# A hybrid decoder step on one core: a sample's value window put together in DRAM, parts of the first tokens ahead of their squares, constants cast later

## The chip, the core and the metric

The kernel runs on one core of a Trainium2 chip. The core has TensorE (PE; its weight loads are shown apart as PEld), VectorE (DVE), ScalarE (ACT), GpSimd (POOL) and SyncE (SP). In this kernel SP computes nothing: it issues all the DMAs of the program, in one queue. 16 DMA engines move the data. The metric is device time in microseconds (us), lower is better; a result is the median of several runs.

## The reference

One inference step of a two-layer trunk with model width 1024, for a prompt of 2048 tokens behind 16 learned meta tokens, and for 8 sample sequences of one token each. Layer 0 projects the normed input and feeds two branches: attention in a window of 128 with a learned sink for each head, and a gated delta rule in chunks behind a short convolution; both are gated and projected together. Layer 1 is gated linear attention. What the change touches is the samples' attention in layer 0. Its window is the 128 youngest keys and values; the oldest of the cache drops out and the new one comes in, and the window that is used is also an output:

```python
    k = jnp.concatenate([k_buf.astype(k_new.dtype), k_new], axis=1)
    v = jnp.concatenate([v_buf.astype(v_new.dtype), v_new], axis=1)
    ...
    mask = (diff >= 0) & (diff < WINDOW)
    o = _sink_attend(q.reshape(Bn, T, A_KV_HEADS, A_GROUP, A_HEAD_DIM), k, v, mask, sink)
    return o.reshape(Bn, T, A_HEADS, A_HEAD_DIM), k[:, T:], v[:, T:]
```

So for each of the 8 samples the value window is rows 1 to 127 of its cache and one new row, each row 128 numbers of float32 (512 bytes).

## The kernel before

The tokens are cut into four groups of 512 columns; the first also carries the 8 sample tokens and the 16 meta tokens in front (536 columns, `CMAX`). For each group the kernel runs layer 0 and layer 1 (`ab_head`, `ab_rest`, `c_main`, `c_out`). Every large product is made of three: weights and activations are split into a rounded part (`hi`, on ACT) and the rest (`lo`, on DVE), and hi x hi, hi x lo and lo x hi are summed in PSUM. In the first group the weights come raw from DRAM and are split (`load_w`, L270 to L278), and their parts are stored in DRAM (L245) for the later groups, which load them (L258). Eight buffers (`NW`) hold weights, and each block of 128 output columns takes three of them: raw, hi, lo. Four PSUM buffers (`pp`) take the large products, four others (`pc`) the small ones. General tiles in SBUF come from a ring of 52 (`ft`).

The order of emission is written by hand. `bulk` emits the large products and between them steps of side streams (generators that yield an estimated wait), chosen by a clock of estimated PE time: delta-rule chunks (`dn_head`), pairs of attention heads (`swa_pair`), the samples' work (`dn_sample`, `swa_extra`). `join` emits what is left of streams before going on. Dependences and semaphores are set by the framework, which also reorders instructions: one that is ready early may be issued ahead of others on its engine, and so do loads that need nothing. On each engine, and in SP's DMA queue, the order so found is then fixed: what stands behind a waiting instruction waits too.

The start (L132 to L226). The gains `PV`, the first eight x tiles `X0`, the first weights `w0` and the constants `CC` are loaded. A loop over the eight tiles makes hi (ACT, L149) and lo (DVE, L150) and adds the squares into `acc0` (ACT L152 or L155, DVE L156). Then small constants are cast or computed: `identb`, `negb` and `triu` (masks and identity in other types), `nsink`, `nea` (an exponential on ACT, L183), `WU` (three steps from the loaded `w_gku`) and `SEL`. `ab_first` makes the row scales `rbn` from `acc0`; `ab_head` then projects K (`ab_k`), whose results are multiplied by `rbn` and copied into the key tiles `kh`, and starts the first convolution head (`ab_conv`), in which the value projection `ab_v` runs.

The samples' values. In `ab_v` (slot "e") the values of the 24 extra tokens are evicted to `e` (named `exv`); `vm` and a part of `BA` are copied from it by DMA (L701, L702), and `vs` (8 partitions x 128) by DVE (L705). `swa_extra` runs beside the last head pair of the first group. It loads, for two halves of four samples, the key window `kc` (transposed, 128 partitions, L495) and the value window `vc`, where the partition is the position in the window: 127 partitions from the cache (L498), the 128th from `vs` (L499). It then computes scores (L527), copies them (L531), softmax, transposes (L542), multiplies by `vc` and stores the result as columns of `M`. Last, it writes the output `vs`: 127 rows from cache to output (L563) and the new row (L564).

Behind it `ab_out` makes the output projection in two parts: first the heads that are ready (`kts[0]`, two of eight, 256 columns of weights), with the residual x loaded by L991 and added in the eviction (`ev_1`, a line of the helper at L115), then, after `join(q.dn + q.sw + xs)`, the other six (`ev_2`).

Of the kernel before, what the change touches and what calls it, by code (L numbers as in the profile page):

```python
# [9 lines left out]
F32 = mybir.dt.float32  # L10
# [10 lines left out]
SMP = 8  # L21
# [47 lines left out]
def kernel(ctx: ExitStack, tc: tile.TileContext, ins, outs):  # L69
# [16 lines left out]
    def const(shape, dt=F32, name="c"):  # L86
        n = nm(name)
        return cp.tile(shape, dt, tag=n, name=n)

    def ft(dt=F32, shape=(128, CMAX)):  # L90
        return wk.tile(list(shape), dt, tag="T", bufs=NT, name=nm("t"))
# [19 lines left out]
    def TT(out, a, b, op, eng=None):  # L111
        (eng or V).tensor_tensor(out, a, b, op=op)  # L112

    def STT(out, a, s, b, op0, op1):
        V.scalar_tensor_tensor(out, a, s, b, op0=op0, op1=op1)  # L115

    def TS(out, a, s1, s2=None, op0=ALU.mult, op1=None):
        if op1 is None:
            V.tensor_scalar(out, a, s1, None, op0=op0)  # L119
        else:  # L120
            V.tensor_scalar(out, a, s1, s2, op0=op0, op1=op1)
# [24 lines left out]
    for kt in range(8):  # L146
        hi, lo = hl(), hl()
        gk = PV[:, P_GAB + kt:P_GAB + kt + 1]
        A.activation(hi, X0[kt], AF.Copy, scale=gk)  # L149
        STT(lo, X0[kt], gk, hi.bitcast(F32), mul, sub)  # L150
        if kt == 0:
            A.activation(acc0, X0[kt], AF.Square)  # L152
        else:
            sq = ft()
            A.activation(sq, X0[kt], AF.Square)  # L155
            TT(acc0, acc0, sq, add)  # L156
        H0[0].append(hi)
        H0[1].append(lo)
    RV = const([128, 16], name="RV")
    SY.dma_start(RV, ins["rowv"].to_broadcast([128, 16]))  # L160
    ident = CC[:, C_ID:C_ID + 128]
# [4 lines left out]
    idc = CC[:, C_IDC:C_IDC + 32]  # L166
    mrow = CC[:, C_MR:C_MR + 1]
    identb = const([128, 128], BF16, "identb")
    V.tensor_copy(identb, ident)
    negb = const([128, 128], BF16, "negb")  # L170
    ngr = ft(shape=(128, 128))
    SY.dma_start(ngr, ins["negm"])
    V.tensor_copy(negb, ngr)
    triu = const([128, 128], U32, "triu")
    V.tensor_copy(triu, tri)
    ones = const([128, 128], name="ones")
    V.memset(ones, 1.0)
    mh = const([128, 1], name="mh")
    V.memset(mh, -0.5)
    nsink = const([128, 8], name="nsink")  # L180
    TS(nsink, RV[:, 0:8], -1.0)
    nea = const([128, 4], name="nea")
    A.activation(nea, RV[:, 8:12], AF.Exp)  # L183
    TS(nea, nea, -1.0)
    dtb = RV[:, 12:16]

    def rpow(out, x):
        G.tensor_tensor(out, x, mh[0:x.shape[0]].to_broadcast(list(x.shape)), op=ALU.pow)  # L188


    WU = const([96, 512], F32R, "WU")
    wur = ft(shape=(128, 512))
    SY.dma_start(wur[0:16, :], ins["w_gku"])
    V.memset(WU.bitcast(F32), 0.0)
    V.tensor_copy(WU[0:16], wur[0:16, :])
    V.tensor_copy(WU[32:48], wur[0:16, :])
    TT(WU[64:80], wur[0:16, :], WU[0:16].bitcast(F32), sub)


    Sdn = []  # L200
# [14 lines left out]

    GS = GR = const([96, 640], F32R, "GS")
    V.memset(GS.bitcast(F32), 0.0)
    SEL = const([96, 4], F32R, "SEL")
    V.memset(SEL.bitcast(F32), 0.0)
    V.tensor_copy(SEL[0:4], ident[0:4, 0:4])  # L220
    V.tensor_copy(SEL[32:36], ident[32:36, 32:36])
    junk = const([128, 256], BF16, name="junk")

    AMK = const([128, 4, 128], name="AMK")
# [246 lines left out]
    def swa_extra(q, gx):  # L471
        vt = q.vt

        vm, vs = vt["m"], vt["s"]
        sc = cb()
        for h in range(8):
            MM(sc[0:16, 16 * h:16 * h + 16], QX[:, h, SMP:EX], KX[:, h // 4, SMP:EX])
        S3 = t512((128, 8, 16))[0:16]
        TT(S3, sc[0:16, 0:128].rearrange("p (h k) -> p h k", h=8), bcm(CC[0:16, C_MSK + 128:C_MSK + 144], 8), add)
        st = sm((128, 32))[0:16]  # L480
        V.tensor_reduce(st[:, 0:8], S3, axis=AX.X, op=amax)
        TT(st[:, 0:8], st[:, 0:8], RV[0:16, 0:8], amax)
        TT(S3, S3, bc(st[:, 0:8], 16), sub)
        A.activation(S3, S3, AF.Exp)
        TT(st[:, 8:16], RV[0:16, 0:8], st[:, 0:8], sub)
        A.activation(st[:, 8:16], st[:, 8:16], AF.Exp)
        V.tensor_reduce(st[:, 16:24], S3, axis=AX.X, op=add)
        TT(st[:, 16:24], st[:, 16:24], st[:, 8:16], add)
        V.reciprocal(st[:, 24:32], st[:, 16:24])
        TT(S3, S3, bc(st[:, 24:32], 16), mul)  # L490
        yield from take_in("T", 5)
        kc, vc = ([ft(shape=(128, 4, 128)) for _ in range(2)] for _ in range(2))
        for x in range(2):
            b4 = slice(4 * x, 4 * x + 4)
            SY.dma_start(kc[x][:, :, 0:127], ins["kcT"][:, b4])  # L495
            for kv in range(2):
                V.tensor_copy(kc[x][64 * kv:64 * kv + 64, :, 127], KX[:, kv, 4 * x:4 * x + 4])
            SY.dma_start(vc[x][0:127], ins["cv"][b4, 1:128, :].rearrange("b k d -> k b d"))  # L498
            SY.dma_start(vc[x][127:128, :, :], vs[4 * x:4 * x + 4, :])  # L499
        QZ = ft(shape=(128, 512))  # L500
        V.memset(QZ, 0.0)
        for kv in range(2):
            r = slice(64 * kv, 64 * kv + 64)
            dst = QZ[r, 0:504].rearrange("p (b x) -> p x b", x=72)[:, 4 * kv:4 * kv + 4, :]
            V.tensor_copy(dst, QX[:, 4 * kv:4 * kv + 4, 0:7])
            V.tensor_copy(QZ[r, 504 + 4 * kv:508 + 4 * kv], QX[:, 4 * kv:4 * kv + 4, 7])
        yield LAT["sx_1"], 0.3
        pt = cb()
        for h in range(8):
            T.transpose(pt[0:16, 16 * h:16 * h + 16], S3[:, h, :], ident[0:16, 0:16])  # L510
        PT = t512((128, 128))[0:16]
        A.copy(PT, pt[0:16, 0:128])
        yield LAT["sx_2"], 0.3
        po = cb()
        for kv in range(2):
            MM(po[64 * kv:64 * kv + 64, 0:64], vm[0:16, 64 * kv:64 * kv + 64], PT[:, 64 * kv:64 * kv + 64])
        yield from until(lambda: gx)
        for u in range(4):
            z = t512((128, 16))
            TT(z, po[:, 16 * u:16 * u + 16], GX[:, u, SMP:EX], mul)  # L520
            store_m0(q, u, z, SMP, META)

        yield 0.5, 0.1

        sc = cb()
        for b in range(8):
            MM(sc[0:64, 0:128], QZ[:, 64 * b:64 * b + 64], kc[b // 4][:, b % 4], start=(b == 0), stop=(b == 7))  # L527
        P = t512((128, 128))[0:64]
        st = sm((128, 8))[0:64]
        snk = PV[0:64, P_SNK:P_SNK + 1]  # L530
        V.tensor_copy(P, sc[0:64, 0:128])  # L531
        V.tensor_reduce(st[:, 0:1], P, axis=AX.X, op=amax)
        TT(st[:, 0:1], st[:, 0:1], snk, amax)
        TS(st[:, 1:2], st[:, 0:1], -1.0)
        A.activation(P, P, AF.Exp, bias=st[:, 1:2], accum_out=st[:, 2:3])
        A.activation(st[:, 3:4], snk, AF.Exp, bias=st[:, 1:2])
        TT(st[:, 2:3], st[:, 2:3], st[:, 3:4], add)
        V.reciprocal(st[:, 4:5], st[:, 2:3])
        TS(P, P, st[:, 4:5])
        yield LAT["sx_3"], 0.9  # L540
        pt = cb()
        T.transpose(pt[:, 0:64], P, ident[0:64, 0:64])  # L542
        PT = t512((128, 64))
        A.copy(PT, pt[:, 0:64])
        yield LAT["sx_4"], 0.1
        po = cb()
        for b in range(8):
            MM(po[:, 8 * b:8 * b + 8], vc[b // 4][:, b % 4], PT[:, 8 * b:8 * b + 8])
        pos = t512((128, 64))
        A.copy(pos, po[:, 0:64])  # L550
        pv = pos.rearrange("p (b h) -> p h b", b=8)
        for u in range(4):
            z = t512((128, 8))
            for kv in range(2):
                r = slice(64 * kv, 64 * kv + 64)
                TT(z[r], pv[r, 4 * kv + u, :], GX[r, u, 0:SMP], mul)
            store_m0(q, u, z, 0, SMP)

        give("T", 5)
        yield LAT["sx_5"], 0.9  # L560

        SY.dma_start(outs["ks"][:, 0:127, :], ins["ck"][:, 1:128, :])
        SY.dma_start(outs["vs"][:, 0:127, :], ins["cv"][:, 1:128, :])  # L563
        SY.dma_start(outs["vs"][:, 127, :], vs[0:8, :])  # L564
        kt_ = cb()
        for kv in range(2):
            T.transpose(kt_[0:8, 64 * kv:64 * kv + 64], KX[:, kv, 0:SMP], ident[0:64, 0:64])
        kn = t512((128, 128))[0:8]
        A.copy(kn, kt_[0:8, 0:128])
        SY.dma_start(outs["ks"][:, 127, :], kn)  # L570
# [110 lines left out]
    def ab_v(q):  # L681
# [7 lines left out]
        def ev_v(p2, slot):  # L689
# [6 lines left out]
            if slot == "e":  # L696
# [6 lines left out]
                V.tensor_copy(BA[0:SMP, 5, :], e[0:SMP, 128:136])  # L703
                vs = wk.tile([128, 128], F32, tag="va", bufs=6, name=nm("vs"))
                V.tensor_copy(vs[0:SMP], e[0:SMP, 0:128])  # L705
                q.vt["m"], q.vt["s"] = vm, vs
            else:
                t = wk.tile([128, 128], F32, tag="va", bufs=6, name=nm("va"))
# [250 lines left out]

    def ab_head(q):  # L960
        bulk(ab_k(q))
        ab_conv(q, 0)

    def ab_rest(q):
# [914 lines left out]
```

## Time and profile before

| | |
|---|---|
| median of 3 runs | 2248.47 us (2241.6 to 2253.84) |
| the profiled execution | 2245.83 us |
| its span in the profile | 2244.0 us |
| busy share of PE, PEld | 96%, 81% |
| busy share of DVE, ACT, POOL | 55%, 37%, 12% |
| DMA, mean | 178 GB/s |
| granted PE clock, mean | 0.985 |

The page of the profile gives one execution. Busy shares are averages over the span; the span in 40 slices of 56 us shows where an engine is less busy:

```profile
PE   7899987999999999999999999999999999999997
...
PEclk9999998999999999999999999999999999999998
```

Each digit is the busy share, and the clock that was granted to PE, in tenths. The slices that matter here are the first and those from 280 to 390 us (the sixth and seventh), all in the first group. In the views that follow L12 is a line of the kernel; L109, L112, L115, L119 and L121 are helpers (`MM`, `TT`, `STT`, `TS`), so their rows are told apart by the tiles they write and read. "SPq" rows are DMA issues of SP with the time that the issue held its queue, not the transfer.

### The profile page before, as it was taken

How to read it: one execution, taken by the hardware profiler on the slowest of the kernel's cores; microseconds unless marked ns; L12 is line 12 of the kernel's file. 1: busy time of each engine (PE TensorE's matmuls, PEld its weight loads, DVE VectorE, ACT ScalarE, POOL GpSimd, SP SyncE). 2: the span in 40 equal slices, each digit the busy share in tenths (PEclk: the TensorE clock that was granted, in tenths of full speed). 3: DMA queues.
4: the chain of work that ended last, by engine and by line, in shares of the span. 5: the costliest groups of instructions: out<-in, count | busy, mean ns of one | idle time of the engine just before them, and what ended most of it. 6: DMA issues, size and time to landing. Idle time of an engine off the chain costs nothing.

```text
span 2244.0 us, 43751 instructions
## 1 busy us (share of the span) xinstructions
PE 2155.2 (96%) x17290; PEld 1809.1 (81%) x17290; DVE 1231.4 (55%) x3501; ACT 836.4 (37%) x2235; POOL 264.3 (12%) x314
## 2 busy tenths in 40 slices
PE   7899987999999999999999999999999999999997
PEld 6788877988888877788887877778887877778886
DVE  6778865665565466545344466544335366654323
ACT  4445443443353244334333244334233233334222
POOL 0011100021200011002130110002130001001111
PEclk9999998999999999999999999999999999999998
DMA  6553425858766732364554743274554653274444
GB/s 215 187 193 130 155 84 182 298 181 285 256 229 219 259 120 98 126 216 168 188 186 154 251 141 114 89 253 152 177 187 158 227 176 115 78 257 159 159 147 155
DMA packets 162568, 399.65 MB, mean 178 GB/s; under 512 B 22010, under 2 KB 54426, under 8 KB 162346
## 3 DMA queue, kind: packets, MB, share of 16 engines
q1 hardware_dynamic: 162362, 396.84, 52.0%
q8 instruction: 136, 2.23, 0.4%
q14 instruction: 70, 0.57, 0.1%
HBM read 296.67 MB, written 101.17 MB: 177 GB/s over the span
## 4 chain that ended last, share of the span: by engine, by line
PE 68%; DVE 5%; DMA 2%; issue 2%; ACT 2%; POOL 1%; SPq 0%; DVEq 0%; POOLq 0%; ACTq 0%
PE pp L109 51%; PE pc L109 13%; DVE t L115 2%; DVE t L112 1%; DVE inv L112 1%; PE pc L931 1%; PE pc L1710 1%; DMA t<-x2d 1%; POOL sm L188 0%; DMA t<-in_xT 0%; DVE t L119 0%; DMA raw<-in_w_cv 0%; DVE t L915 0%; DMA raw<-in_w_co 0%; ACT t L920 0%
## 5 line engine op out<-in xcount | busy, mean ns | idle before, releaser
L109 PE MATMUL pp<-t,wh 128*128 128x512 f32 (+1 forms) x4528 | 1267.7, 364 | 32.8 <-DVE t L115 13.3
L109 PEld LDWEIGHTS pp<-t,wh 128*128 128x128 f32 x4528 | 782.1, 190 | 144.6 <-DVE t L115 14.1
L109 PE MATMUL pp<-t,wl 128*128 128x512 f32 (+1 forms) x2264 | 810.4, 359 | 3.1 <-DVE wl L112 3.1
L109 PEld LDWEIGHTS pp<-t,wl 128*128 128x128 f32 x2264 | 430.0, 190 | 62.9 <-DVE wl L112 3.8
L112 POOL TENSOR_TENSOR t<-t,t 128x512 fp32r<-128x512 f32 (+3 forms) x128 | 163.7, 1295 | 526.4 <-ACT t L587 295.2
L109 PE MATMUL pp<-wh,t 128*128 128x256 f32 (+1 forms) x1088 | 208.6, 288 | 3.8 <-DVE QKt L112 3.8
L115 DVE SCALAR_TENSOR_TENSOR t<-t,PV,t 128x512 f32<-128x512 f32 (+4 forms) x232 | 176.7, 769 | 59.4 <-ACT t L1012 26.7
L109 PEld LDWEIGHTS pp<-wh,t 128*128 128x128 f32 x1088 | 171.8, 190 | 6.1 <-DVE QKt L112 4.0
L115 DVE SCALAR_TENSOR_TENSOR t<-pp,t 128x512 f32<-128x512 f32 (+3 forms) x160 | 93.2, 586 | 135.8 <-PE pp L109 64.9
L188 POOL TENSOR_TENSOR sm<-sm,mh 128x2 f32<-128x2 f32 (+3 forms) x84 | 68.5, 815 | 825.3 <-DVE sm L115 373.0
L109 PE MATMUL pp<-wl,t 128*128 128x256 f32 (+1 forms) x544 | 155.4, 286 | 0.0
L112 DVE TENSOR_TENSOR wl<-raw,wh 128x512 fp32r<-128x512 f32 (+3 forms) x138 | 92.3, 688 | 22.3 <-ACT wh L275 11.3
L109 PEld LDWEIGHTS pp<-wl,t 128*128 128x128 f32 x544 | 103.4, 190 | 0.7
L275 ACT CAST wh<-raw 128x512 fp32r<-128x512 f32 (+2 forms) x122 | 67.7, 587 | 77.3 <-DMA raw<-in_w_c 20.7
L112 DVE TENSOR_TENSOR t<-t,t 128x512 f32<-128x512 f32 (+4 forms) x103 | 62.9, 613 | 40.4 <-ACT t L399 38.7
L112 DVE TENSOR_TENSOR QKt<-pp,t 128x512 f32<-128x512 f32 (+1 forms) x40 | 23.2, 586 | 111.6 <-PE pp L109 101.0
L109 PEld LDWEIGHTS pc<-t,t 128*128 128x128 f32 (+4 forms) x496 | 63.0, 162 | 23.4 <-ACT t L1507 5.1
L920 ACT ACTIVATE t<-t,sm 128x257 f32<-128x257 f32 x128 | 64.1, 504 | 45.0 <-DVE sm L115 44.2
L109 PE MATMUL pc<-t,t 128*128 128x128 f32 (+5 forms) x496 | 78.0, 267 | 2.4 <-ACT t L1507 1.1
L399 ACT ACTIVATE t<-t 128x512 f32<-128x512 f32 (+1 forms) x70 | 44.1, 630 | 90.2 <-DVE t L115 67.5
L112 DVE TENSOR_TENSOR t<-pp,t 128x268 f32<-128x268 f32 (+1 forms) x90 | 44.5, 496 | 53.3 <-PE pp L109 38.2
L933 ACT COPY t<-pc 128x512 f32<-128x512 f32 x64 | 37.4, 585 | 75.1 <-PE pc L931 74.9
(334 smaller groups left out, 2808.5 us busy)
## 6 DMA issues: line engine op xcount, KB each, us to landing
wh<-wd SPq DMA_DIRECT2D x157, 512.0 KB, 3.7
wl<-wd SPq DMA_DIRECT2D x157, 512.0 KB, 4.5
wd<-wh SPq DMA_DIRECT2D x55, 512.0 KB, 4.4
wd<-wl SPq DMA_DIRECT2D x55, 512.0 KB, 3.7
t<-in_xT SPq DMA_DIRECT2D x72, 256.0 KB, 4.7
raw<-in_w_ab SPq DMA_DIRECT2D x25, 512.0 KB, 4.8
raw<-in_w_c SPq DMA_DIRECT2D x16, 512.0 KB, 4.5
out_yp<-t SPq DMA_DIRECT2D x32, 256.0 KB, 2.7
```

The costliest lines, as they stand in the source:

```text
L109: T.matmul(out, lhsT, rhs, start=start, stop=stop)
L112: (eng or V).tensor_tensor(out, a, b, op=op)
L115: V.scalar_tensor_tensor(out, a, s, b, op0=op0, op1=op1)
L188: G.tensor_tensor(out, x, mh[0:x.shape[0]].to_broadcast(list(x.shape)), op=ALU.pow)
L275: A.copy(hi[:, c], raw[:, c])
L399: A.activation(sq[:, :q.C], x, AF.Square)
L920: A.activation(S_[:, kv], S_[:, kv], AF.Exp, bias=st[:, 2 + kv:3 + kv], accum_out=st[:, 4 + kv:5 + kv])
L931: T.transpose(pt[:, kv, x], S_[:, kv, 128 * x:128 * x + 128], ident)
L933: A.copy(PT, pt)
L1710: T.transpose(oT[:, c], On[:, c, 128 * j:128 * j + 128], ident)
```

## The change

Three things are changed. (a) In the loop over the first tiles all eight pairs of parts come first, and a second loop makes the squares. (b) The casts of constants move into a function `late_constants`, called for the first group between the K projection and the first convolution head; each of its computing instructions is pinned behind what was emitted before it on its engine. The two loads that they need (`negm`, `w_gku`) move with them; the memsets stay. (c) A DRAM tile `vwin` of 8 x 128 x 128 is filled in `ab_v`: 127 rows of each sample from the cache, the new row from `vs`. `swa_extra` loads its value windows from it, with 128 partitions, and the output `vs` is copied from it.

```diff
@@ the first tiles @@
         STT(lo, X0[kt], gk, hi.bitcast(F32), mul, sub)
+        H0[0].append(hi)
+        H0[1].append(lo)
+    for kt in range(8):
         if kt == 0:
             A.activation(acc0, X0[kt], AF.Square)
         else:
             sq = ft()
             A.activation(sq, X0[kt], AF.Square)
             TT(acc0, acc0, sq, add)
-        H0[0].append(hi)
-        H0[1].append(lo)
@@ constants @@
-    V.tensor_copy(identb, ident)
-    ngr = ft(shape=(128, 128))
-    SY.dma_start(ngr, ins["negm"])
-    V.tensor_copy(negb, ngr)
-    V.tensor_copy(triu, tri)
-    TS(nsink, RV[:, 0:8], -1.0)
-    A.activation(nea, RV[:, 8:12], AF.Exp)
-    TS(nea, nea, -1.0)
+    def late_constants():
+
+        pin = tc.keep_in_program_order
+        ngr = ft(shape=(128, 128))
+        SY.dma_start(ngr, ins["negm"])
+        wur = ft(shape=(128, 512))
+        SY.dma_start(wur[0:16, :], ins["w_gku"])
+        pin(A.activation(nea, RV[:, 8:12], AF.Exp))
+        pin(V.tensor_scalar(nea, nea, -1.0, None, op0=mul))
+        pin(V.tensor_copy(identb, ident))
+        pin(V.tensor_copy(negb, ngr))
+        pin(V.tensor_copy(triu, tri))
+        pin(V.tensor_scalar(nsink, RV[:, 0:8], -1.0, None, op0=mul))
+        pin(V.tensor_copy(SEL[0:4], ident[0:4, 0:4]))
+        pin(V.tensor_copy(SEL[32:36], ident[32:36, 32:36]))
+
+        pin(V.tensor_copy(WU[0:16], wur[0:16, :]))
+        pin(V.tensor_copy(WU[32:48], wur[0:16, :]))
+        pin(V.tensor_tensor(WU[64:80], wur[0:16, :], WU[0:16].bitcast(F32), op=sub))
-    wur = ft(shape=(128, 512))
-    SY.dma_start(wur[0:16, :], ins["w_gku"])
-    V.tensor_copy(WU[0:16], wur[0:16, :])
-    V.tensor_copy(WU[32:48], wur[0:16, :])
-    TT(WU[64:80], wur[0:16, :], WU[0:16].bitcast(F32), sub)
-    V.tensor_copy(SEL[0:4], ident[0:4, 0:4])
-    V.tensor_copy(SEL[32:36], ident[32:36, 32:36])
@@ swa_extra @@
-            SY.dma_start(vc[x][0:127], ins["cv"][b4, 1:128, :].rearrange("b k d -> k b d"))
-            SY.dma_start(vc[x][127:128, :, :], vs[4 * x:4 * x + 4, :])
+            SY.dma_start(vc[x], q.vwin[b4].rearrange("b k d -> k b d"))
...
-        SY.dma_start(outs["vs"][:, 0:127, :], ins["cv"][:, 1:128, :])
-        SY.dma_start(outs["vs"][:, 127, :], vs[0:8, :])
+        SY.dma_start(outs["vs"], q.vwin)
@@ ab_v @@
                 V.tensor_copy(vs[0:SMP], e[0:SMP, 0:128])
+
+                q.vwin = dr.tile([8, 128, 128], F32, tag="vwin", bufs=1, name=nm("vwin"))
+                SY.dma_start(q.vwin[:, 0:127, :], ins["cv"][:, 1:128, :])
+                SY.dma_start(q.vwin[:, 127, :], vs[0:SMP])
@@ ab_head @@
         bulk(ab_k(q))
+        if q.g == 0:
+            late_constants()
         ab_conv(q, 0)
```

More of the change, by code (lines that the diff above doesn't have):

```diff
@@ L180 @@
     nsink = const([128, 8], name="nsink")
-    TS(nsink, RV[:, 0:8], -1.0)
     nea = const([128, 4], name="nea")
-    A.activation(nea, RV[:, 8:12], AF.Exp)
-    TS(nea, nea, -1.0)
     dtb = RV[:, 12:16]
+    WU = const([96, 512], F32R, "WU")
+    V.memset(WU.bitcast(F32), 0.0)
+    SEL = const([96, 4], F32R, "SEL")
+    V.memset(SEL.bitcast(F32), 0.0)
+    def late_constants():
[15 more added lines that the diff above has]
+        pin(V.tensor_tensor(WU[64:80], wur[0:16, :], WU[0:16].bitcast(F32), op=sub))
     def rpow(out, x):
         G.tensor_tensor(out, x, mh[0:x.shape[0]].to_broadcast(list(x.shape)), op=ALU.pow)
-    WU = const([96, 512], F32R, "WU")
-    wur = ft(shape=(128, 512))
-    SY.dma_start(wur[0:16, :], ins["w_gku"])
-    V.memset(WU.bitcast(F32), 0.0)
-    V.tensor_copy(WU[0:16], wur[0:16, :])
-    V.tensor_copy(WU[32:48], wur[0:16, :])
-    TT(WU[64:80], wur[0:16, :], WU[0:16].bitcast(F32), sub)
     Sdn = []
@@ L217 @@
     V.memset(GS.bitcast(F32), 0.0)
-    SEL = const([96, 4], F32R, "SEL")
-    V.memset(SEL.bitcast(F32), 0.0)
-    V.tensor_copy(SEL[0:4], ident[0:4, 0:4])
-    V.tensor_copy(SEL[32:36], ident[32:36, 32:36])
     junk = const([128, 256], BF16, name="junk")
```

## The prediction

> **What bounds the kernel now.** I read the busy shares first, then the waits by engine, then the time line wherever TensorE (PE) waits. PE is busy 96% of the span, so a part of the program counts only where PE stands still. Of the waits of PE between 296 and 420 us one is large; columns: engine and line, what it waited for, us in total, times, longest.
>
> ```profile
> PE pp L109 <- DVE t L115: 13.0, 1, 13.0
> PE pp L109 <- DVE wl L112: 2.9, 2, 2.8
> ```
>
> It stands in the first group, where the first part of the output projection begins (`ab_out`) while the sample's attention (`swa_extra`) and the last head pair still run. The time line (start, length, engine, line, operation) shows who makes it:
>
> ```profile
> 328.97 0.27 PE L109 MATMUL pc<-t,t 128*64 128x128 f32 x1
> 329.03 0.65 PE L109 MATMUL pc<-t,va 128*64 128x128 f32 x7
> ...
> 342.23 0.44 DVE L115 SCALAR_TENSOR_TENSOR t<-pp,t 128x268 f32<-128x268 f32 x1 [13.87 <-DMA t<-in_xT]
> ...
> 342.73 0.82 PE L109 MATMUL pp<-t,wh 128*128 128x268 f32 x2 [13.05 <-DVE t L115]
> 342.73 0.28 DVE L531 COPY t<-pc 64x128 f32<-64x128 f32 x1
> ```
>
> PE stops at 329.7 with its PSUM buffers full; VectorE (DVE) can't empty them because the residual x (`in_xT`, L991) hasn't come. That load was issued late, and the queue of SP says why:
>
> ```profile
> 309.92 1.37 SPq L495 DMA_DIRECT2D t<-in_kcT  x1
> 311.35 0.36 SPq L498 DMA_DIRECT2D t<-in_cv  x1
> 311.75 11.99 SPq L499 DMA_DIRECT2D t<-vs  x1
> 323.79 0.44 SPq L495 DMA_DIRECT2D t<-in_kcT  x1
> 324.27 0.36 SPq L498 DMA_DIRECT2D t<-in_cv  x1
> 324.69 13.16 SPq L499 DMA_DIRECT2D t<-vs  x1
> 337.94 0.39 SPq L991 DMA_DIRECT2D t<-in_xT  x1
> 338.43 0.38 SPq L270 DMA_DIRECT2D raw<-in_w_abo  x1
> ```
>
> Both issues of L499, which move only 2 KB each, hold SP for 11.99 and 13.16 us, 25.15 together, and everything behind them in the queue too: the x loads and the next weights. What they stand behind is the load of L498, as the DMA view from 311.7 to 324 us shows (40 slices of 0.31 us):
>
> ```profile
> GB/s 10 84 249 319 177 8 12 22 22 22 22 22 22 22 22 20 20 20 18 20 20 20 20 20 20 20 45 20 20 20 20 20 20 18 20 20 20 20 20 20
> ...
> t<-in_kcT SPq DMA_DIRECT2D x1, 254.0 KB, 4.3
> ```
>
> The 254 KB of `in_kcT`, to 128 partitions, pass in four slices at up to 319 GB/s. The 254 KB of `in_cv`, to 127 partitions, trickle at about 20 GB/s until SP is released: 254 KB at 20.5 GB/s is 12.4 us, between the two times of L499. So I read L499 as held up by the 127-partition load ahead of it, not as slow by itself. [...]
>
> After the stall the granted clock stays low (columns: stretch, length, busy of PE, PEld, DVE, ACT, POOL, then PE clock, DMA share, GB/s):
>
> ```profile
> 330.00:343.00 13.00, 0.28 (x1) 0.28 (x2) 0.77 (x5) 0.41 (x1) 0.00 (x0) 0.68 0.28 79
> ...
> 343.00:350.00 7.00, 7.00 (x41) 6.47 (x41) 3.97 (x18) 1.37 (x5) 0.00 (x0) 0.62 0.42 135
> ...
> 343.00:376.50 33.50, 28.39 (x177) 24.07 (x178) 21.31 (x93) 11.01 (x34) 1.28 (x1) 0.77 0.46 140
> ```
>
> **The change, part by part.** *Value rows.* Both L498 and both L499 go; one load per half from `q.vwin` comes, to 128 partitions with the shape of L495, which SP issued in 0.44 and 1.37 us. SP is thus free for the x loads some 25 us earlier. That isn't the gain: PE had other work until 329.7. What follows the stall hangs on the sample's scores, whose copy (L531) DVE does at 342.73 behind the blocked eviction. The last matmul of these scores ends at 328.97 + 0.27 = 329.24, so with x there the copy runs at about 329.2: **-13.5 us**. From the copy to the second part of the output projection it is a chain of the sample's softmax and the last head pair:
>
> ```profile
> 310.52 0.71 PE L109 MATMUL pc<-kh,t 128*128 128x256 f32 x4
> ...
> 325.27 0.75 PE L109 MATMUL pc<-kh,t 128*128 128x256 f32 x4
> ...
> 350.81 0.72 PE L109 MATMUL pc<-kh,t 128*128 128x256 f32 x4
> ...
> 368.31 0.73 PE L109 MATMUL pc<-kh,t 128*128 128x256 f32 x4
> ...
> 374.33 0.75 PE L109 MATMUL pp<-t,wh 128*128 128x268 f32 x4 [0.35 <-ACT wh L275]
> ```
>
> 342.73 to 374.33 is 31.6 us. How much of it goes with the low clock is open from 0 (all of it latency of DVE and ACT) to 28.39 x (1 - 0.77) = 6.5 us (all of it PE). The pair before went from its first to its fourth block of scores in 325.27 - 310.52 = 14.8 us at full clock, this one needs 368.31 - 350.81 = 17.5: 2.7 longer. Of the 8.1 us ahead of it (342.73 to 350.81) PE is busy throughout at 0.62, but the softmax chain fills most. I take **-3 us** in all, a little under half. [...]
>
> The preparing DMAs, by their nearest rows:
>
> ```profile
> 9.95 2.92 SPq L562 DMA_DIRECT2D out_ks<-in_ck  x1
> ...
> 21.94 0.74 SPq L563 DMA_DIRECT2D out_vs<-in_cv  x1
> ...
> 40.86 0.59 SPq L701 DMA_DIRECT2D vm<-exv  x1
> ...
> 94.44 0.33 SPq L564 DMA_DIRECT2D out_vs<-vs  x1
> ...
> 94.00:98.00 4.00, 4.00 (x47) 3.24 (x46) 3.44 (x17) 1.14 (x2) 0.00 (x0) 1.00 0.67 262
> ```
>
> The block into `vwin` is L563 with another destination and needs nothing that is computed, so it can go as early; the row into `vwin` is L564 moved to where `vs` is made. SP already stands until 40.86 for the tile from which `vs` is copied, so 0.33 us more delay the weights behind it by that and no more; PE works on the value projection then. New is one copy `vwin` to `out_vs`, 512 KB read and written, 0.74 to 2.92 us of SP and 1.05 MB / 262 GB/s = 4 us of DMA. It may be issued once the row has landed, soon after 41 us; L564 went at 94, where PE is 4.00 of 4.00 us busy and that work hides it: 0. Without that cover it costs up to 4 us. The new waits on `vwin` end some 250 us before `swa_extra` reads it: 0.
>
> *Parts ahead of squares, late casts.* PE's first wait ends with the first parts either way. What holds it next is the sum of squares, the K evictions and the value weights:
>
> ```profile
> 13.57 0.21 ACT L183 ACTIVATE nea<-RV 128x4 f32<-128x4 f32 x1 [1.36 <-DMA RV<-in_rowv]
> ...
> 15.68 0.22 DVE L169 CAST identb<-CC 128x128 bf16<-128x128 f32 x1
> ...
> 17.63 0.16 DVE L221 CAST SEL<-CC 4x4 fp32r<-4x4 f32 x1
> ...
> 29.16 0.42 DVE L195 CAST WU<-t 16x512 fp32r<-16x512 f32 x1
> ...
> 30.04 0.68 DVE L112 TENSOR_TENSOR WU<-t,WU 16x512 fp32r<-16x512 f32 x1
> ...
> 35.13 12.96 PE L109 MATMUL pp<-wv,t 128*128 128x272 f32 x80 [5.38 <-DVE wv L112]
> ```
>
> ACT stands 1.36 us for `RV` and works 0.21 ahead of the squares of the last tiles: 1.6 us go. On DVE six small casts (15.68 to 17.79, 0.16 to 0.22 each, about 1.1 together) leave the way to the sum of squares. They return behind the K evictions, where the three WU steps (0.42, 0.42, 0.68) already stand, and delay the value weights for which PE waits at 35.13: +1.1. The order of parts and squares moves the same work about; the sum of squares is ready when all of it is done. The moved loads `negm` and `w_gku` are small and SP is idle from 22.7 to 40.86. Bounds: -2 (all gained, the casts hidden in DVE's waits) to +1.1 (nothing gained); I take **-0.5**.
>
> Sum: -13.5 - 3 - 0.5 = **-17 us**. The profiled execution took 2245.83 us (span 2244.0), so 2228.8 by its own time; it lies 0.12% below the median of the runs, 2248.47, to which the same 17 us give **2231 us**.
>
> **Rivals.** For the first, two weight loads ahead of the stall, with a third between them:
>
> ```profile
> 286.00 0.45 SPq L270 DMA_DIRECT2D raw<-in_w_abo  x1
> ...
> 306.72 0.35 SPq L270 DMA_DIRECT2D raw<-in_w_abo  x1
> ```
>
> (1) *The wait is shortened, not removed.* With eight weight buffers and three used by each block of 128 columns, the weights of the fourth block can't be loaded until the first is multiplied, whatever SP does; the stage stays thin, the clock low, and the 2.8 us wait on `wl` stays as another one. For it: that row. Against: three blocks were issued by 306.72, which is work for PE until the fourth comes. Gain 13.0 - 2.8 = 10.2, 2238 us. (2) *The stage becomes bound by PE's work.* 28.39 us at 0.77 is 21.9 at full clock; from 329.7 that ends at 351.6 instead of 376.5: -25, 2223 us. Against: the head pair's 14.8 us between blocks even at full clock. (3) *The change doesn't do what it says.* If loads of 512-byte rows from DRAM in this order are slow whatever the partitions, the new load trickles as well, and the next issue stands behind it: 0, 2248 us. For it: the value load differs from the K load in order too. Against: 20 GB/s is a sixteenth of 319. (4) *Slower.* The new copy `vwin` to `out_vs` is one unbroken run and is put on one engine: 524 KB at 20 GB/s is 26 us, and SP, held as at L499, hands PE no weights; with the few microseconds of weights that eight buffers hold, PE would lose some 22 us, and 3 more by the clock: +25 - 17 = +8, 2256 us. It decides if the copy is on fewer than about two engines. Against it: L563, also DRAM to DRAM, is followed by full-rate traffic, and its shape (8 rows) is the same but for one row in 128. [...]
>
> **How the numbers follow.** Forecast 0.64 (its own range 2226 to 2236), rival 1 0.18, rival 2 0.06, rival 3 0.07, rival 4 0.05. A measurement of this kernel tells about 0.5% (11 us) from no change, that is 2237: the forecast, rival 2 and somewhat under half of rival 1 are faster, 0.78; the rest of rival 1 and rival 3 the same, 0.17; rival 4 slower, 0.05. The range 2222 to 2240 holds the forecast, rival 1 and half of rival 2; the open costs (0 to 6.5 of clock, -2 to +1.1 at the start, 0 to 4 of the copy) lie in it.
>
> **What would show it.** Right: no SP issue of over 3 us near 311 us; the x loads issued before 320; no wait of PE on DVE L115 of over 3 us there; the granted clock above 0.9 where it was 0.77; the second part of the output projection about 17 us earlier against its start, and everything behind it shifted by that alone. The start: PE's matmuls on the value weights within 2 us of 35.1. Wrong: a load from `vwin` that trickles at 20 GB/s, a long issue behind the copy to `out_vs`, or a new wait of PE on `raw<-in_w_abo`.

## The result, and the profile after

| | before | after |
|---|---|---|
| median | 2246.8 us of 4 runs (2241.6 to 2253.84) | 2225.5 us of 4 runs (2222.36 to 2226.02) |
| the profiled execution | 2245.83 us, span 2244.0 | 2226.02 us, span 2224.2 |
| granted PE clock, mean | 0.985 | 0.988 |

The ratio after to before is 0.99, with a 95% interval of 0.9871 to 0.993. The changed kernel is faster, by 21.3 us between the medians and by 16 to 29 us (0.7% to 1.29% of 2246.8) with the interval. Between the two profiled executions the span is 19.8 us shorter. The forecast was 17 us and 2231: the measured 2225.5 lies inside the range of 2222 to 2240, and half a us below the forecast's own 2226 to 2236.

The waits of PE between 290 and 420 us, to be held against the first fence of the prediction (engine and line, what it waited for, us in total, times, longest):

```profile
PE pp L109 <- DVE wl L112: 1.7, 2, 1.5
PE pc L109 <- ACT t L939: 1.5, 2, 0.7
```

The 13.0 us on DVE L115 is gone, and these two are the largest that are left. The reason stands in SP's queue, in the time line of the changed kernel (L499 is now the key window, L502 the value window, L999 the residual x, L274 the raw weights):

```profile
310.65 0.43 SPq L499 DMA_DIRECT2D t<-in_kcT  x1
311.13 1.38 SPq L502 DMA_DIRECT2D t<-vwin  x1
312.61 0.45 SPq L499 DMA_DIRECT2D t<-in_kcT  x1
313.10 0.51 SPq L502 DMA_DIRECT2D t<-vwin  x1
313.71 0.45 SPq L999 DMA_DIRECT2D t<-in_xT  x1
320.39 0.35 SPq L274 DMA_DIRECT2D raw<-in_w_abo  x1
...
324.87 0.42 SPq L999 DMA_DIRECT2D t<-in_xT  x1
```

No issue here holds SP for more than 1.38 us. The first x load leaves at 313.71 instead of 337.94. The DMA view from 309 to 324 us (40 slices of 0.375 us) shows that the value windows, with one more partition each, don't trickle:

```profile
GB/s 52 55 292 3 0 161 208 60 201 305 129 123 216 304 289 323 313 315 379 349 193 34 11 0 0 0 0 0 0 0 22 0 3 106 235 5 0 0 0 0
...
t<-vwin SPq DMA_DIRECT2D x2, 256.0 KB
```

What hung on the stall comes earlier. The same four steps as in the prediction, from the time line: the copy of the sample's scores (now L534), the first and fourth block of the last head pair's scores, and the second part of the output projection:

```profile
329.55 0.28 DVE L534 COPY t<-pc 64x128 f32<-64x128 f32 x1
...
335.84 0.73 PE L109 MATMUL pc<-kh,t 128*128 128x256 f32 x4
...
352.86 0.73 PE L109 MATMUL pc<-kh,t 128*128 128x256 f32 x4
...
358.56 0.76 PE L109 MATMUL pp<-t,wh 128*128 128x268 f32 x4
```

To see where the 19.8 us came from, I take the start of the same DMA issue of SP in both executions, along the program:

| issue | before | after | shift |
|---|---|---|---|
| weights of the output projection, ahead of the stage | 286.00 | 286.70 | +0.7 |
| first store to `x1d`, just behind the stage | 381.31 | 365.52 | -15.8 |
| first store to `x2d` | 691.61 | 677.16 | -14.4 |
| first store to `out_yp` | 762.53 | 748.05 | -14.5 |
| first store to `x1d` of the second group | 967.86 | 950.01 | -17.9 |
| of the third | 1480.15 | 1461.81 | -18.3 |
| of the fourth | 1993.48 | 1973.89 | -19.6 |

The stage alone gives -15.8 - 0.7 = -16.5. Behind it, where the change touches nothing, the shift moves on: 1.3 us are lost up to the first `x2d` store, 3.4 are won between 762 and 968, and 1.7 more in the next two groups. The section on the prediction comes back to that.

### The profile page after: what moved, and what is told of

The parts are those of the page before. It is cut to its first block, busy times and chain, and to the rows that moved or that the text cites. A ratio compares the mean times of both kernels' runs of the same rounds, so it can differ in the third digit from the quotient of the medians.

```text
span 2224.2 us, 43755 instructions
## 1 busy us (share of the span) xinstructions
PE 2151.2 (97%) x17290; PEld 1807.1 (81%) x17290; DVE 1232.5 (55%) x3501; ACT 836.7 (38%) x2235; POOL 264.5 (12%) x314
## 4 chain that ended last, share of the span: by engine, by line
PE 69%; DVE 5%; DMA 2%; ACT 2%; issue 2%; POOL 1%; SPq 0%; DVEq 0%; POOLq 0%; ACTq 0%
PE pp L109 52%; PE pc L109 13%; DVE t L115 1%; DVE t L112 1%; DVE inv L112 1%; PE pc L937 1%; DMA t<-in_xT 1%; DMA raw<-in_w_cv 1%; PE pc L1718 1%; POOL sm L205 0%; DVE t L119 0%; DVE t L921 0%; DMA t<-x2d 0%; ACT t L926 0%; PE pc L1497 0%
## 5 line engine op out<-in xcount | busy, mean ns | idle before, releaser
L115 DVE SCALAR_TENSOR_TENSOR t<-t,PV,t 128x512 f32<-128x512 f32 (+4 forms) x232 | 175.3, 765 | 58.5 <-ACT t L1020 26.4
L115 DVE SCALAR_TENSOR_TENSOR t<-pp,t 128x512 f32<-128x512 f32 (+3 forms) x160 | 93.3, 586 | 121.5 <-PE pp L109 71.1
```

## The experiments

Theory A follows the prediction's reading: the load to 127 partitions passes through about one of the 16 DMA engines (an estimate from the trace of before: from 314 to 323 us, where it trickles, the packets of the DMA queue took 7.1% of the time of the 16, at 21 GB/s, which is the time of 1.1 engines), whichever issue is next in SP's queue waits until it has drained, and the whole gain comes from the value window having 128 partitions; the edits at the start are worth nothing. The rivals: B, the 2 KB row load out of `vs` (SBUF to SBUF, one partition) is slow by itself; C, it matters where the window lies (input or DRAM tile), not its shape; D, the start pays a good part of the gain.

**Each part alone.** `e1_values` takes the value rows alone: of the diff above only the pieces in `swa_extra` and `ab_v`. `e2_start` takes the rest alone: the loops and `late_constants`.

```diff
@@ e1_values, against before @@
+                SY.dma_start(q.vwin[:, 0:127, :], ins["cv"][:, 1:128, :])
+                SY.dma_start(q.vwin[:, 127, :], vs[0:SMP])
...
-            SY.dma_start(vc[x][0:127], ins["cv"][b4, 1:128, :].rearrange("b k d -> k b d"))
-            SY.dma_start(vc[x][127:128, :, :], vs[4 * x:4 * x + 4, :])
+            SY.dma_start(vc[x], q.vwin[b4].rearrange("b k d -> k b d"))
```

> The value rows alone (part c); start and casts as before. Theory (the gain is the end of the hold of SP in the first group): about 17 to 20 us below the kernel before, PE's 13.0 us wait gone, the second part of the output projection begins some 16.5 us earlier against the program's start. Rival (the reordered start brings a good part of the 21 us): at most 12 us below before.

Measured: 2224.27 us (2220.99 to 2231.03, 6 runs), ratio to before 0.9905 with the interval 0.9884 to 0.9927. That is the whole gain.

> Parts a and b alone (squares after the parts, late casts); the value rows as before. Theory: within 3 us of the kernel before, both L499-type issues still hold SP for 12 and 13 us and PE still waits about 13 us. Rival (the start matters): 8 us or more below before.

Measured: 2244.07 us, ratio 0.9996 (0.9982 to 1.0011): no difference. Its queue still has the two long issues, and PE the stall; SP's time line of `e2_start`:

```profile
310.63 12.32 SPq L503 DMA_DIRECT2D t<-vs  x1
...
323.88 12.72 SPq L503 DMA_DIRECT2D t<-vs  x1
```

Rival D falls: with this interval the start is worth at most 0.2%, some 4 us. The profiled executions fit: `e2_start` reaches its first `out_yp` store at 760.63, 1.9 us ahead of before's 762.53, `e1_values` at 747.02, 15.5 ahead.

**Which property of the load.** `e3_split` keeps the kernel before, with the row from `vs`, and only cuts the 127 partitions into 112 and 15. `e4_127` keeps the changed kernel and does the opposite: the window comes from `vwin`, but as 127 partitions and one.

```diff
@@ e3_split, against before @@
-            SY.dma_start(vc[x][0:127], ins["cv"][b4, 1:128, :].rearrange("b k d -> k b d"))
+            SY.dma_start(vc[x][0:112], ins["cv"][b4, 1:113, :].rearrange("b k d -> k b d"))
+            SY.dma_start(vc[x][112:127], ins["cv"][b4, 113:128, :].rearrange("b k d -> k b d"))
@@ e4_127, against after @@
-            SY.dma_start(vc[x], q.vwin[b4].rearrange("b k d -> k b d"))
+            SY.dma_start(vc[x][0:127], q.vwin[b4, 0:127, :].rearrange("b k d -> k b d"))
+            SY.dma_start(vc[x][127:128], q.vwin[b4, 127:128, :].rearrange("b k d -> k b d"))
```

> The kernel before, with the cache load of 127 partitions cut into one of 112 and one of 15; the row load from vs stays as it is. Theory (the load of 127 partitions runs on one engine and holds whatever is issued behind it): no issue of over 3 us near 311 us, the time within 4 us of the value rows alone, so 14 to 20 us below before. Rival (the row load from vs is slow by itself, 4 partitions into 1): both row loads still take 12 to 13 us of SP, time as before.

Measured: 2231.94 us (2221.95 to 2232.75, 4 runs), ratio 0.9922 (0.9891 to 0.9952). SP's time line of `e3_split` (L498 and L499 are the two pieces of the window, L500 is the row):

```profile
313.39 0.50 SPq L498 DMA_DIRECT2D t<-in_cv  x1
313.93 0.50 SPq L499 DMA_DIRECT2D t<-in_cv  x1
314.48 0.67 SPq L500 DMA_DIRECT2D t<-vs  x1
...
316.23 0.50 SPq L499 DMA_DIRECT2D t<-in_cv  x1
316.78 0.59 SPq L500 DMA_DIRECT2D t<-vs  x1
317.48 0.38 SPq L992 DMA_DIRECT2D t<-in_xT  x1
```

The row load that held SP for 11.99 and 13.16 us takes 0.67 and 0.59 once the load ahead of it is cut in two. Two DMAs more, and the hold is gone: rival B falls. The time was expected 14 to 20 us below before and came out 12.5 below (2244.45 in these runs); the section on the prediction says where the profiled execution loses the difference.

> The changed kernel, but the window is loaded from the DRAM tile as 127 partitions and one. Theory: the hold comes back with the 127 partitions, an issue of 11 to 13 us behind each, and PE's wait of some 13 us; 15 to 20 us above the changed kernel. Rival (the source in DRAM or the row from vs matters): no long issue, time as the changed kernel.

Measured: 2244.52 us, ratio 0.9992 (0.9976 to 1.0007): the gain is gone. SP's time line of `e4_127` (L502 is the piece of 127 partitions, L503 that of one, both from `vwin`):

```profile
313.17 0.36 SPq L502 DMA_DIRECT2D t<-vwin  x1
313.57 11.82 SPq L503 DMA_DIRECT2D t<-vwin  x1
...
325.92 0.35 SPq L502 DMA_DIRECT2D t<-vwin  x1
326.32 12.74 SPq L503 DMA_DIRECT2D t<-vwin  x1
339.16 0.39 SPq L1000 DMA_DIRECT2D t<-in_xT  x1
```

and the wait of PE is back, in the waits of `e4_127`:

```profile
PE pp L109 <- DVE t L115: 12.5, 1, 12.5
```

One partition fewer costs the whole gain, some 20 us against `e1_values`, from the same tile in DRAM: rival C falls.

**Who is held.** `e7_norow` leaves the row loads out of the kernel before, so that the load of 127 partitions has no small DMA behind it. It leaves the new value rows out of the samples' attention: the 128th row is set to zero.

```diff
@@ e7_norow, against before @@
+            G.memset(vc[x], 0.0)
             SY.dma_start(vc[x][0:127], ins["cv"][b4, 1:128, :].rearrange("b k d -> k b d"))
-            SY.dma_start(vc[x][127:128, :, :], vs[4 * x:4 * x + 4, :])
```

> The kernel before without the row load from vs (the 128th value row of each sample is zero, set by GpSimd ahead of the load; the samples' attention leaves the new value out). Theory (SP is held at whatever it issues next, once the 127-partition load is queued): the second load of kcT and the first load of x are held for 11 to 13 us each in place of the row loads, PE waits 12 to 13 us. Rival (only a second write into the same tile is held): no issue of over 3 us, PE's wait gone, about 15 us less.

Measured: 2248.5 us, a single run. SP's time line of `e7_norow` (L495 is the key window, L499 the value window, L991 the residual x):

```profile
308.44 1.33 SPq L495 DMA_DIRECT2D t<-in_kcT  x1
315.95 0.27 SPq L499 DMA_DIRECT2D t<-in_cv  x1
316.31 11.35 SPq L495 DMA_DIRECT2D t<-in_kcT  x1
327.72 0.83 SPq L499 DMA_DIRECT2D t<-in_cv  x1
328.64 12.87 SPq L991 DMA_DIRECT2D t<-in_xT  x1
```

The hold moves to whatever comes next: 11.35 us at the second key window, which takes 0.44 us in the prediction's rows, and 12.87 at the x load, which took 0.39. PE's wait on DVE L115 is 11.7 us here. The memset on GpSimd came late and kept the first window from going out until 315.95 (SP stands for 6 us), so the total of this run isn't a measure of anything; the five rows are.

**The start, taken apart.** The changed kernel has two edits there. `e5_squares` is the value rows with the squares in a second loop, `e6_late` the value rows with `late_constants`; `e8_later` is the changed kernel with `late_constants` called later still, at the end of `ab_v`, in the hope that the value weights come first.

```diff
@@ e8_later, against after: in ab_head @@
-        if q.g == 0:
-            late_constants()
@@ and at the end of ab_v @@
+                late_constants()
```

> Value rows and squares behind the parts (c and a), casts of constants as before. Theory (the start gives nothing; its waits only change places): time within 4 us of the value rows alone (2224 us), PE's wait on the value weights near 5.5 us instead of 8.6. Rival (the squares bring something that the late casts take back): 4 us or more below the value rows alone.

Measured: 2230.49 us (2227.51 to 2232.98, 6 runs), ratio 0.9931 (0.9911 to 0.995).

> Value rows and late casts (c and b), squares beside the parts as before. Theory: within 4 us of 2224 us; PE's wait on the value weights near 8.6 us, since the casts lie ahead of them on DVE. Rival (the longer wait comes from the squares): the wait stays near 5.5 us.

Measured: 2225.09 us (2224.06 to 2227.26, 5 runs), ratio 0.9909 (0.989 to 0.9928).

> The changed kernel with the late casts called at the end of the value projection, where DVE waits for PE anyway. If the casts ahead of the value weights cost what the trace shows, PE's wait on the value weights falls from 8.6 to about 5.5 us and the time lies 0 to 4 us below the changed kernel (0.1%, hardly to be told); if other waits take its place, it is the same.

Measured: 2227.45 us (2225.81 to 2230.67, 6 runs), ratio 0.9921 (0.9903 to 0.9939): no gain over the changed kernel.

None of the three is clearly better than the changed kernel. `e5_squares` missed its expectation: it lies 6.2 us above the value rows alone, and above `e6_late` in every run. What the start does is read from two things in the profiled executions: when PE begins its matmuls on the value weights (`wv`), and what PE waits for in the first 160 us.

| version | squares behind | late casts | `wv` matmuls begin | wait on `wv` | other waits of over 2 us but for the first parts' |
|---|---|---|---|---|---|
| before | no | no | 35.13 | 5.4 | 7.8 on `wh` |
| `e3_split` | no | no | 35.12 | 5.6 | 7.8 on `wh` |
| `e1_values` | no | no | 34.59 | 5.8 | 4.9, 2.6 |
| `e2_start` | yes | yes | 37.09 | 8.9 | 3.7, 2.7 |
| `e5_squares` | yes | no | 37.82 | 5.4 | 5.3, 2.6, 2.3 on `wh` |
| `e6_late` | no | yes | 37.92 | 10.2 | 4.7, 2.6 |
| `e8_later` | yes | yes, later | 37.96 | 8.3 | 5.0, 2.6 |
| after | yes | yes | 38.41 | 8.6 | 4.5, 2.6 |

The late casts lengthen the wait on `wv`, by 3 to 5 us. But the matmuls begin later with either edit, by 2.7 us in `e5_squares` and 2.8 in `e6_late`: in `e5_squares` the K evictions ahead of them come later, and the wait itself stays at 5.4. `e8_later` didn't mend it, and missed the 5.5 us that it was to show. Its time line has the late casts at 52.9 us, far behind the split of `wv`; but three steps of the first convolution head (L115, 2.38 us together) and one more (0.71) now stand ahead of that split, as the same three do in the other versions with late casts.

## Why the prediction was right, and where it was not

**The cause.** Right, and shown from both sides: behind a load to 127 partitions the next issue is held, be it a row, a key window or an x load (11.82 and 12.74 us in `e4_127`, 11.35 and 12.87 in `e7_norow`); behind loads to 112 and 15, or to 128, the same issues are not (0.67 and 0.59 us for the row in `e3_split`, 0.45 for the key window and the x load in after). From the first weights of the output projection to the first `x1d` store the four profiled executions with the hold take 92.2 to 99.0 us (before, `e2_start`, `e4_127`, `e7_norow`), the six without it 77.7 to 79.3. The prediction read L499 as held rather than slow; L500 of `e3_split`, the same instruction at 0.67 and 0.59 us, is that reading as a measurement. (The view's 254 KB are 4 x 127 x 512 bytes, 260 thousand, so at 20.5 GB/s the load takes 12.7 us and not 12.4; that too lies between the two holds.) Rival 3 of the prediction (512-byte rows trickle whatever the partitions) fell with the DMA view of after (up to 379 GB/s). That it is about one engine for 127 partitions stays an estimate, from the 7.1% of before: between 313 and 317 us of after, while loads to 128 pass, the mean busy share of the 16 engines was 0.89, at 266 GB/s. The engines themselves were counted in no run, and why the load to 127 gets so few isn't shown. What the runs show is the hold on the next issue, and that the loads to 112 and 15 hold nothing (0.50 to 0.67 us for each issue of `e3_split`).

**The term of -13.5.** The copy of the scores was put at about 329.2. It ran at 329.55, that is 13.18 us ahead of 342.73, and 13.9 ahead once the 0.7 by which the whole program was later at 286 us is taken off. Right.

**The term of -3.** From the copy to the second part it is 358.56 - 329.55 = 29.0 us, against 31.6: -2.6, inside the bounds of 0 and 6.5. Of this, 1.8 us lie between the copy and the first block of the last pair's scores (335.84 - 329.55 = 6.3 instead of 8.1), 0.5 between the first and the fourth (17.0 instead of 17.5) and 0.3 behind that. Size right, but the reason was only half right. The windows of the changed kernel (stretch, length, busy of PE, PEld, DVE, ACT and POOL, then PE clock, DMA share, GB/s):

```profile
331.00:336.00 5.00, 4.87 (x41) 4.22 (x40) 2.88 (x12) 1.37 (x5) 0.00 (x0) 1.00 0.50 162
336.00:340.00 4.00, 3.84 (x19) 3.08 (x19) 3.52 (x17) 1.29 (x4) 1.27 (x1) 0.58 0.36 102
340.00:345.00 5.00, 2.51 (x17) 1.94 (x18) 4.29 (x24) 2.23 (x7) 0.00 (x0) 0.84 0.80 240
345.00:350.00 5.00, 5.00 (x22) 4.10 (x20) 2.32 (x8) 1.16 (x5) 0.00 (x0) 0.50 0.34 111
350.00:355.00 5.00, 4.49 (x35) 3.76 (x35) 3.45 (x18) 1.98 (x6) 0.00 (x0) 0.97 0.13 44
```

The prediction asked for a clock above 0.9 where it was 0.77. It is 1.00 in the 5 us where the old kernel came out of its stall at 0.62, and there the 1.8 us are. Behind it the clock falls to 0.58 and 0.50 with no pause of PE longer than 1.5 us ahead, so the mean from 331 to 360 us is 0.82. That step failed: I took all of the low clock from 343 to 376 us for a consequence of the stall. Finer windows of the kernel before show that it was two dips:

```profile
343.00:345.00 2.00, 2.00 (x11) 2.00 (x11) 2.00 (x11) 0.00 (x0) 0.00 (x0) 0.50 0.43 106
...
349.00:351.00 2.00, 2.00 (x19) 2.00 (x18) 0.29 (x1) 0.01 (x1) 0.00 (x0) 1.00 0.00 0
...
354.00:356.00 2.00, 0.00 (x0) 0.00 (x0) 1.97 (x12) 0.17 (x2) 0.00 (x0) 0.80 0.53 148
...
361.00:363.00 2.00, 2.00 (x9) 1.69 (x8) 0.00 (x0) 0.81 (x4) 0.00 (x0) 0.50 0.42 132
```

The first (0.50 at 343) is over by 349 to 351 (1.00); the second (0.50 at 361) belongs to the stage and is there in both kernels, in the changed one at 345 to 350. So only the first was the stall's to give back, and the -3 came near by luck: I had taken a little under half of what the clock could give. What makes the second dip wasn't tried, but the traces show what goes with it. In before and in seven of the runs, with the hold or without, PE stands for 2.5 to 2.8 us shortly behind the first block of scores (353.5 to 356.25 in before), and within some 1.3 us of the end of that pause, ahead or behind, a dip of 7 to 10 us begins (in before the clock was 0.50 in the windows from 355.5 to 365). `e3_split`, which has no such pause, has no such dip. The dip of after at 336 to 340, 3.3 us long (0.50 from 337 to 340) with no pause ahead, is in `e3_split` too and in no other trace; what makes it stays open.

**The term of -0.5.** Too small to be told, and wrong in its parts. At the first weights of the output projection, 286 us, the changed kernel is 0.7 us late, inside the bounds of -2 and +1.1. But the same issue stands at 287.39 in `e3_split` and at 284.53 in `e7_norow`, which differ from before (286.00) only behind it, so executions differ by more than 0.7. And the sign that the prediction named, PE's matmuls on the value weights within 2 us of 35.1, failed: the time line of after has

```profile
34.57 0.41 DVE L200 CAST WU<-t 16x512 fp32r<-16x512 f32 x1
...
35.45 0.68 DVE L202 TENSOR_TENSOR WU<-t,WU 16x512 fp32r<-16x512 f32 x1
36.15 1.57 DVE L115 SCALAR_TENSOR_TENSOR t<-t,PV,t 128x528 f32<-128x528 f32 x2
37.63 1.35 DVE L112 TENSOR_TENSOR wv<-raw,wv 128x544 fp32r<-128x544 f32 x2
...
38.41 12.34 PE L109 MATMUL pp<-wv,t 128*128 128x272 f32 x80 [8.55 <-DVE wv L112]
```

3.28 us later than 35.13. The prediction charged the late casts with the 1.1 us of the six that move behind the K evictions. It overlooked the steps of the first convolution head (L115, 0.77 us for one at 33.19 and 1.57 for the two shown), which stood behind the split of `wv` before and now come ahead of it; and it took the squares in a second loop to cost nothing, where `e5_squares` begins these matmuls 2.7 us later. The cost was then given back: the 7.8 us on `wh` in the first 160 us of the kernel before is gone, and 4.5 and 2.6 stand in its place. That exchange comes with either part of the change: `e1_values`, which leaves the start alone, has it (4.9 and 2.6), and so has `e2_start`, which leaves the values alone (3.7 and 2.7); `e3_split`, which has neither part, keeps the 7.8. In SP's queue `e1_values`, `e2_start` and after issue the next weights of that stage ahead of the wait for the extra tokens' values (at 35.20, 38.12 and 21.28 us), before and `e3_split` behind it (42.19 and 42.18); but so does `e8_later` (45.23), without the wait of 7.8, so what makes the exchange stays open.

**Preparing DMAs at 0.** Right: the three stand in the time line of after as

```profile
8.27 0.78 SPq L710 DMA_DIRECT2D vwin<-in_cv  x1
...
45.13 0.43 SPq L711 DMA_DIRECT2D vwin<-vs  x1
...
81.82 0.53 SPq L566 DMA_DIRECT2D out_vs<-vwin  x1
```

and no long issue follows the last, the copy that rival 4 put on one engine. The next issue comes only at 101.55, so more is to be had from the DMA view: from 80 to 100 us it shows traffic up to 85 us and next to none after that (at most 33 GB/s in a slice), so the copy was through in about 3 us and not in 26. That such a copy goes to one engine, the source of rival 4's 26 us, no run shows. Rival 4 falls.

**The other rivals.** Rival 1 (the wait is shortened) fell: all of the 13.0 us went, and the 2.8 us on `wl` came down to 1.5 instead of standing; in `e1_values` it stands at 2.8, and that version is as fast. Rival 2 (bound by PE's work) fell too: 29.0 us from the copy to the second part, not the 21.9 of work. The x loads before 320 came only in part: the first at 313.71, the second at 324.87, behind weights that wait for a buffer; no one waits for it.

**The rest of the sum.** The stage gave the 16.5 us that its two terms had promised. The prediction wanted everything behind it shifted by that alone, and that failed: the shift is -15.8, -14.4, -17.9 and -19.6 at four places on the way. The largest step is the 3.4 us between the first `out_yp` store and the second group's first `x1d` store. That stretch takes 205.3 us in the profiled execution of before, 204.5 in that of `e1_values` and 205.7 in that of `e5_squares`, and 201.2 to 202.2 in the seven others, `e2_start`, `e4_127` and `e7_norow` with the long hold among them. So it doesn't follow the value window. The three slow ones have in common what can be seen in before, first in the waits, then in the windows:

```profile
PE pc L109 <- issue: 1.7, 1, 1.7
...
780.00:800.00 20.00, 18.26 (x272) 12.93 (x271) 8.13 (x27) 4.11 (x16) 0.00 (x0) 0.91 0.54 186
```

PE stands once for 1.4 to 1.7 us for nothing that the profile shows, and the clock of the 20 us around it is 0.91 or less (0.83 in `e5_squares`). The other seven have neither, after among them: 20.00 us busy at 1.00 in the same stretch, 14.5 us earlier. Why PE stops there stays open. The stretch makes 3.7 of the 5.6 us by which the profiled execution of `e5_squares` is behind that of `e6_late`. `e3_split` reaches its first `x1d` store at 365.06, level with after, and the first `x2d` store at 682.15, 5.0 us behind it; that is where its profiled execution falls behind. Its clock there is 0.96 from 403 to 443 and from 483 to 563 us, where that of after is 1.00; the cause of that was not followed.

## What to carry to other kernels

When a DMA issue holds its queue for microseconds, look at the DMA ahead of it first: here the culprit issued in 0.36 us, and the instruction with the long bar (11.99 us) was a bystander. The load to 127 partitions was better made to 128, or as two loads (112 and 15): 2225.5 us (after) and 2231.94 (`e3_split`) against 2244.52 with 127 (`e4_127`). The price wasn't the transfer itself but everything queued behind it, here the x load for which PE stood 13 us. And read a low clock in short windows before giving all of it to the nearest stall: one of two dips here was the stall's (0.50 from 342.7 to 348.3 us in before).

## What was not expected of the hardware

- The hold lies on the next issue, whatever it moved here: 11.99 and 13.16 us on 2 KB (before), 11.82 and 12.74 (`e4_127`), 11.35 on a 254 KB key window and 12.87 on an x load (`e7_norow`). It doesn't lie on the slow load's own issue (0.27 to 0.83 us in the same traces).
- The granted clock was 0.50 for 5.00 us in which PE was busy 5.00 (345 to 350 us after), and 1.00 in 331 to 336 with PE busy 4.87 of 5.00. Behind the long stall it came back 5.6 us after PE went on (before, 342.7 to 348.3). The dip to 0.58 at 336 to 340 comes directly behind that busy stretch, in which PE stood for 0.13 us in all, and in eight other traces a pause of 2.5 to 2.8 us went with a dip. Why the clock falls in the dips of the stage, and what brings it back, no run here shows.
